# Attention with three heads instead of two between scores and values, and retention's first tiles in other rooms

## The chip, the cores and the metric

One core of one Trainium2 chip. The core has five engines that run their own instruction queues: PE (TensorE), DVE (VectorE), ACT (ScalarE), POOL (GpSimd) and SP (SyncE, here a queue that issues transfers). The metric is the device time of one execution in microseconds (us), as the median of several runs. Lower is better.

## The reference, cut to what matters

The program is one layer of a decoder with three branches (retention, pooling, sparse attention) for 1024 prompt tokens and 8 x 8 sample tokens. What the change touches is the prompt's attention and the beginning of retention:

```python
s_s = einsum('nqgrd,ngqsd->ngqrs', qb, k_selected) + bias_s     # 8 heads, 64 channels each
p_s = masked_softmax(s_s, dist >= 0)
o_s = einsum('ngqrs,ngqsd->nqgrd', p_s, v_selected)
s_w = einsum('nqgrd,nsgd->nqgrs', qb, k_window) + bias_w         # the last 512 positions
p_w = masked_softmax(s_w, valid_w)
o_w = einsum('nqgrs,nsgd->nqgrd', p_w, v_window)
o   = g0 * o_cmp + g1 * o_s + g2 * o_w
...
z = rms_norm(x, gain) @ w_in
q = rotary(q, pos); k = rotary(k, pos) * dk ** -0.5              # retention, 4 heads, chunks of 128
att = (q @ k.T) * dmask; o = att @ v + (q @ s) * cross; s = s * decay + (k * tail).T @ v
```

## The kernel before, in words

Every large product runs as three f16 products (high x high, high x low, low x high), so weights and activations are kept as pairs of f16 tiles, "h" and "l".

**Attention.** `prompt_attention` (L704) goes over 64 heads: 8 query tiles i of 128 rows, in each 8 heads (2 groups g of 4). With i the number of key blocks grows from 1 to 8 for the selected branch and from 1 to 5 for the window branch. For one head there are three steps.

- `head_scores` (L822): PE multiplies queries and keys into PSUM (L841, L853, L862), DVE adds the bias into an f32 tile `S` (L847, L873) and keeps the maxima, ACT makes the exponent's offset `nm` (L867).
- `head_probs` (L740), for the window branch first and then the selected one: ACT takes the exponentials (L750, L751), DVE or ACT writes their f16 half into `hl`, POOL subtracts to get the other half (L756), and SP issues a transposing transfer from `hl` to `pt` (L758), so that the keys come to lie on the partitions. `hl` and `pt` have 2 rooms for each branch (NHL, NPT).
- `head_values` (L766): PE multiplies `pt` by the values into `o` (L769 and L787, both by way of L1322 to L1324).

Step n of the loop holds the scores of head n, the values of head n - LAG, the weights of head n - 1 and then some steps of the generator `fill`. LAG is 2, and `S` has 3 rooms. After every fourth head `head_norm` (L876) divides on DVE and adds on POOL (L881 to L884); `head_out` (L887) turns that on PE (L891) and gates it. Once per query tile `cmp_attention` (L790) does the compressed branch.

**Fill.** `fill` is a chain of two projections of the input, `silu_c` for retention's gate and `early_gates` (L307 to L309). One step is three matmuls. They need nothing of the attention, and they stand between the heads so that PE has work; each output part goes through a small tile `th` (L932, L1200) of the pool `attw`, and that of `early_gates` from there to memory (`egd`, L1201). By the quota, 24 of the 360 steps are left behind the last head. They follow `head_out` in the program.

**Retention.** `retention` (L1124) loads the weights of its first head (`load_r`, L264, on the ACT queue, in 8 parts of 128 rows), then small tables and the table `rope` of sines and cosines (L1138, L1140, 1.1 MB, on the SP queue), and goes over 4 heads of 9 token tiles. For each, PE makes `z` (L286 to L288, 24 matmuls), `ret_tile` (L1223) rotates it on DVE (L1238 to L1240), after ACT has once per head scaled the table (L1233); SP turns the result (`qt`, L1256), and PE makes the chunk's scores `at` and, two stages later, the output `ro`. `z` has 3 rooms.

**Rooms.** Pools are stacked in SBUF; one that closes leaves its bytes to the next. Per partition, and above what stays: the attention's keys, queries and tables take the first 54.7 KB (`attc` 11.8, `attk` 32.8, `attb` 10.1), its working tiles `attw` lie above. After it, `smc` takes the first 12.4 KB, then come retention's weights `rw` (two rooms of a pair, 32.8 KB, to 45.1), its tables `rc` (23.2 KB, to 68.3; `rope` is 18.4 KB of that), and its working tiles. A tile in a reused room waits for the last user of just those bytes (`reuse_waits="tile"`).

**Order.** Each engine's queue runs in order. Which order that is, a planner decides when the program is built: by a model of the durations it takes, for each engine, the earliest instruction of the program that the model holds ready. So PE may have fill steps ahead of values that the model still waits for, and the order is kept on the chip whatever the true times are. `issue_after(x)` ties what follows to come behind x on x's engine.

Of the kernel before, what the change touches and what calls it, by code (L numbers as in the profile page):

```python
# [11 lines left out]
F32 = mybir.dt.float32  # L12
F16 = mybir.dt.float16
# [7 lines left out]
P = 128  # L21
# [5 lines left out]
N_EARLY, N_FILL = 8, 7  # L27
# [8 lines left out]

FILL_A, FILL_B = 0.2, 3.6

LAG = 2
ND = (1, 2, 3, 4, 5, 6, 7, 8)  # L40
NHL, NPT = 2, 2

# [20 lines left out]
C_RG = 2048  # L63
# [4 lines left out]
C_NG = 5400  # L68
# [59 lines left out]
class Kern:  # L128
# [32 lines left out]
    def run(self):  # L161
        ctx = self.ctx
        right = ExitStack()
        self.setup(ctx)
        with ExitStack() as es:
            self.kvstore(es)
            with ExitStack() as e1:
                self.phase_kv(e1)
            rp = self.pool(right, "gate", side="right")
            self.ga = rp.tile([P, 8, NG, 2, 32], F16, tag="ga", name="ga", bufs=1)  # L170
            self.rp = rp
            self.gc = rp.tile([P, 4, NG, 2, 32], F16, tag="gc", name="gc", bufs=1)
            with ExitStack() as e1:
                sp = self.pool(e1, "attw", bufs=2)
                ps = self.pool(e1, "aps", bufs=1, space=PSUM)
                self.pjb = A_PJ
                self.wq = self.nc.scalar
                self.eq = self.nc.scalar
                self.egd = self.dr.tile([8, P, NTOK], F32, name="egd")
                self.cgd = self.dr.tile([8, P, NTOK], F32, name="cgd")  # L180
                with self.behind():
                    deque(self.silu_c(sp, self.gc, C_NG, ps, self.wng), 0)
                fill = chain(self.silu_c(sp, self.ga, C_RG, ps), self.early_gates(sp, ps, range(N_FILL)))
                self.prompt_attention(sp, ps, fill)
                with self.tc.issue_after(self.after.ins):
                    deque(fill, 0)
                self.eq = self.nc.sync
        with ExitStack() as eo:
            self.smc = self.pool(eo, "smc")
            self.pjb = R_PJ  # L190
            with ExitStack() as es:
                self.psb, ppj, psa = [self.pool(es, x, bufs=1, space=PSUM) for x in ("rpsb", "rppj", "rpsa")]
                self.retention(es, ppj, psa, right)
            self.gbp = self.pool(right, "gbp", side="right")
            self.gb = self.gbp.tile([P, 4, NG, 2, 32], F16, tag="gb", name="gb", bufs=1)
            with ExitStack() as es:
                psb, ps, pst = [self.pool(es, x, bufs=1, space=PSUM) for x in ("spsb", "sppj", "spst")]
                sp = self.pool(es, "smp", bufs=1)
                pool = self.pooling(es, ps, pst)
                next(pool)  # L200
                with self.behind():
                    self.sample_attention(sp, psb, pst)
                next(pool, None)
                self.out_weights(self.pool(es, "wout"))
        with ExitStack() as es:
            self.output(es)
        right.close()
        if self.post:
            self.post(self)
# [53 lines left out]

    def load_r(self, pool, h):  # L264

        hi, lo = [pool.tile([P, 8, 512], F16, tag="rw" + x, name=self.nm("rw" + x), bufs=2) for x in "hl"]
        w = self.d["w_in"][0]
        for k in range(8):
            raw = self.wtile([P, 1024], F32, "raw")
            r = slice(k * P, k * P + P)  # L270
            qk = w[r, C_RET:C_RET + 1024].rearrange("p (a h c) -> p a h c", a=2, c=P)[:, :, h, :]
            self.wq.dma_start(raw[:, 0:256].rearrange("p (a c) -> p a c", c=P), qk)
            self.wq.dma_start(raw[:, 256:512], w[r, 1024 + h * 256:1280 + h * 256])
            self.wsplit(hi[:, k, :], lo[:, k, :], raw[:, :512])
        return hi, lo
# [25 lines left out]
    def proj_c(self, out, hi, lo, s0, n, ks=range(8)):  # L301

        nc = self.nc
        for k in ks:
            xh = self.xh[:, k, s0:s0 + n]
            xl = self.xl[:, k, s0:s0 + n]
            nc.tensor.matmul(out, hi[:, k, :], xh, start=(k == 0), stop=False)  # L307
            nc.tensor.matmul(out, hi[:, k, :], xl, start=False, stop=False)  # L308
            nc.tensor.matmul(out, lo[:, k, :], xh, start=False, stop=(k == 7))  # L309

    def evac(self, out, c0, ps, n, m):

# [387 lines left out]
    def prompt_attention(self, sp, ps, fill):  # L700

        order = range(8)
        heads = [(i, g, r) for i in order for g in range(2) for r in range(4)]
        sc, pr, out, oc = {}, {}, None, {}  # L704
        quota = 0.0
        for n in range(64 + LAG):
            if n < 64:
                sc[n] = self.head_scores(*heads[n], sp, ps)
            if n >= LAG:
                i, g, r = heads[n - LAG]  # L710
                if r == 0:
                    self.o = ps.tile([P, 2, 4, 64], F32, tag="o", name=self.nm("o"), bufs=A_O)
                s, nm, l = sc.pop(n - LAG)
                self.head_values(i, g, r, s, pr.pop(n - LAG), self.o, sp, ps)
                if r == 1 and out:
                    self.head_out(*out, sp, ps)
                if r == 3:
                    out = (i, g, self.head_norm(i, g, self.o, l, oc[i], sp))
            if 1 <= n <= 64:
                i, g, r = heads[n - 1]  # L720
                pr[n - 1] = self.head_probs(i, r, sc[n - 1], sp)
            if n < 64:
                i = heads[n][0]
                quota += FILL_A * (i + 1 + min(i + 1, 5)) + FILL_B
                with self.tc.issue_after(self.after.ins):
                    while quota >= 1:
                        next(fill, None)
                        quota -= 1
                if n % 8 == 3:
                    oc[i] = self.cmp_attention(i, sp, ps)  # L730
        self.head_out(*out, sp, ps)

    @staticmethod
    def cuts(i):
# [90 lines left out]
    def head_scores(self, i, g, r, sp, ps):  # L825
        nc = self.nc
        h = 4 * g + r
# [4 lines left out]
        near = min(2, i + 1) * P  # L832
        far_s, far_w = nk - near, nw - near
        nfs = -(-far_s // 512)
        s = sp.tile([P, 1664], F32, tag="S", name=self.nm("S"), bufs=3)

        st = sp.tile([P, 8], F32, tag="hst", name=self.nm("hst"), bufs=4)
        pn = ps.tile([P, 2, 256], F32, tag="s", name=self.nm("pn"), bufs=A_S)
        for br in range(2):
            for hl in range(2):  # L840
                self.after = nc.tensor.matmul(pn[:, br, :near], q, self.kst[:, br * 4 + g * 2 + hl, nk - near:nk],  # L841
                                 start=(hl == 0), stop=(hl == 1))
# [7 lines left out]
        if far_w:  # L850
            pw = ps.tile([P, 512], F32, tag="s", name=self.nm("pw"), bufs=A_S)
            for hl in range(2):
                nc.tensor.matmul(pw[:, :far_w], q, self.kst[:, 4 + g * 2 + hl, w0:w0 + far_w],  # L853
                                 start=(hl == 0), stop=(hl == 1 and i < 4))
# [3 lines left out]
        for c in range(nfs):  # L858
            n = min(512, far_s - 512 * c)
            pf = ps.tile([P, 512], F32, tag="s", name=self.nm("pf"), bufs=A_S)  # L860
            for hl in range(2):
                nc.tensor.matmul(pf[:, :n], q, self.kst[:, g * 2 + hl, 512 * c:512 * c + n], start=(hl == 0),  # L862
                                 stop=(hl == 1))
# [259 lines left out]

    def retention(self, es, ps, psa, right):  # L1124
        nc, d = self.nc, self.d
        rw = self.pool(es, "rw")
        rc = self.pool(es, "rc")
        rp = self.pool(es, "rp", bufs=2)
        lg = np.log1p(-np.exp2(-5.0 - np.arange(4)))
        w = {0: self.load_r(rw, 0)}  # L1130
        self.wq = nc.sync
        self.wp3 = self.pool(right, "wpipe3", side="right")
        rv = rc.tile([P, 2, 2, 4], F32, name="rv")
        nc.sync.dma_start(rv, d["c_rv"])

# [6 lines left out]
        nc.sync.dma_start(mt, d["c_mt"])  # L1142
        mts = rc.tile([64, 4, 64], F32, name="mts")
        nc.sync.dma_start(mts, d["c_mts"])
        c2 = rc.tile([P, 2, 4], F32, name="c2")
        nc.vector.tensor_tensor(c2, rv[:, :, 0, :], rv[:, :, 0, :], op=ALU.mult)
        nc.vector.tensor_scalar(c2, c2, 1.0 / 256, None, op0=ALU.mult)
# [13 lines left out]
        for n in range(len(steps) + NSTAGE):  # L1161
            z = None
            if n < len(steps):
                h, t = steps[n]
                z = ps.tile([P, 512], F32, tag="pj", name=self.nm("z"), bufs=self.pjb)
                self.proj_t(z, *w[h], t, 0, 512)
                if t == 2 and h < 3:
                    with self.behind():
                        w[h + 1] = self.load_r(rw, h + 1)

            for x in reversed(live):
                next(x, None)
            if z is not None:
                live.append(self.ret_tile(rp, psa, h, t, z, env))
            if n > 5:
                with self.behind():
                    next(prep, None)
            if n == len(steps) - 2:
                with self.behind():
                    self.raw0 = [self.sample_rows(self.smc, b) for b in range(2)]  # L1180
# [781 lines left out]
```

## Time and profile before

| | |
|---|---|
| three runs | 1325.66, 1319.22, 1324.78 us; median 1324.78 |
| the profiled execution | 1325.59 us, its span 1323.8 us |
| busy | PE 95%, DVE 68%, ACT 48%, POOL 39% of the span |
| TensorE's granted clock | 0.982 of full speed in the mean |
| prompt attention | about 158 to 507 us of the span |
| retention's first tiles | about 508 to 545 us |

The profile is one execution. A line of a timeline gives start, duration, engine, source line, operation, the tile written <- the tiles read, and in brackets for how long the engine stood before it and what released it. A line of waits gives who waited for whom, us in total, how often, and the longest.

### The profile page before, as it was taken

Reading aid. Unit: us, or ns where it says so; the run is one execution under the profiler, and the core shown is the slowest. Engines: PE = TensorE matmul, PEld = TensorE weight load, DVE = VectorE, ACT = ScalarE, POOL = GpSimd, SP = SyncE. Lnnn points to the kernel's source line nnn. Section 1 sums busy time; section 2 is a strip of 40 time slices with the busy share of each in tenths; the row PEclk is TensorE's granted clock in tenths of the full one; section 3 lists DMA queues with packets and bytes.
Section 4 is the critical chain, followed back from the end, with each engine's and each line's share of the span. In section 5 each row is a group of like instructions: output and inputs, shape, how many; then the busy total and the mean of one; then the engine's idle time right before and its main releaser. Section 6 shows DMA issues by size and latency. Waiting matters only on the chain. (4 is left out here: it accounts for less than half of the span.)

```text
span 1323.8 us, 27839 instructions
## 1 busy us (share of the span) xinstructions
PE 1260.5 (95%) x10520; PEld 853.9 (65%) x10520; DVE 905.6 (68%) x2288; ACT 632.3 (48%) x1474; POOL 518.6 (39%) x561
## 2 busy tenths in 40 slices
PE   7999899999999899899999998998999999999997
PEld 4555566767666664455656565666788888888643
DVE  6647536777767663767675657664588967579975
ACT  5633436766757662555554444344543433212332
POOL 1112013566665661245463560101534466423133
PEclk8999899999999999999999999998999999999998
DMA  7866624678889996252652278326641211543622
GB/s 258 171 129 153 143 64 95 108 134 151 165 156 182 167 189 178 61 151 68 174 133 61 63 212 249 104 50 226 220 144 33 81 49 49 170 138 116 230 97 97
DMA packets 324317, 179.25 MB, mean 135 GB/s; under 512 B 204434, under 2 KB 298610, under 8 KB 323765
## 3 DMA queue, kind: packets, MB, share of 16 engines
q1 hardware_dynamic: 283844, 137.83, 44.2%
q10 hardware_dynamic: 35600, 26.32, 6.8%
q0 software_dynamic: 4736, 13.31, 3.2%
q8 instruction: 82, 1.34, 0.4%
q14 instruction: 55, 0.44, 0.1%
HBM read 98.80 MB, written 33.25 MB: 100 GB/s over the span
## 5 line engine op out<-in xcount | busy, mean ns | idle before, releaser
L756 POOL TENSOR_TENSOR hl<-S,hl 128x640 f16<-128x640 f32 (+7 forms) x128 | 152.6, 1201 | 153.0 <-DVE hl L755 94.0
L307 PE MATMUL pj<-xh,whi 128*128 128x384 f16 (+1 forms) x480 | 154.1, 321 | 4.8 <-ACT ue L1417 4.1
L309 PE MATMUL pj<-xh,wlo 128*128 128x384 f16 (+1 forms) x480 | 153.9, 321 | 0.0
L308 PE MATMUL pj<-xl,whi 128*128 128x384 f16 (+1 forms) x480 | 153.8, 320 | 0.0
L286 PE MATMUL z<-rwh,xh 128*128 128x512 f16 x256 | 97.0, 379 | 0.0
L288 PE MATMUL z<-rwh,xl 128*128 128x512 f16 x256 | 97.0, 379 | 0.0
L287 PE MATMUL z<-rwl,xh 128*128 128x512 f16 x256 | 97.0, 379 | 0.0
L751 ACT ACTIVATE S<-S,nm 128x640 f32<-128x640 f32 (+7 forms) x128 | 93.7, 732 | 4.3 <-DVE gc L934 0.4
L308 PEld LDWEIGHTS <-whi 128*128 128x128 f16 x672 | 66.5, 99 | 38.6 <-issue 8.4
L309 PEld LDWEIGHTS <-wlo 128*128 128x128 f16 x672 | 66.5, 99 | 36.2 <-issue 2.4
L307 PEld LDWEIGHTS <-whi 128*128 128x128 f16 x672 | 66.4, 99 | 34.0 <-issue 2.4
L1566 DVE TENSOR_TENSOR q<-st,q 128x288 f32<-128x288 f32 (+1 forms) x168 | 70.3, 434 | 26.2 <-PE st L1557 25.2
L220 ACT ACTIVATE whi<-raw 128x1024 f16<-128x1024 f32 (+1 forms) x48 | 45.5, 948 | 63.8 <-PE pj L308 14.7
L286 PEld LDWEIGHTS <-xh 128*128 128x128 f16 x448 | 45.4, 101 | 46.2 <-issue 7.0
L1322 PE MATMUL o<-vst,pt 128*128 128x64 f16 x528 | 58.3, 194 | 17.6 <-DMA pt<-hl 17.2
L288 PEld LDWEIGHTS <-xl 128*128 128x128 f16 x448 | 44.1, 98 | 46.1 <-issue 2.1
L847 DVE CUSTOM_DVE_ANT_0 S<-pn,tnear 128x256 f32<-128x256 f32 (+1 forms) x128 | 47.3, 403 | 36.5 <-PE pn L841 32.2
L287 PEld LDWEIGHTS <-xh 128*128 128x128 f16 x448 | 44.0, 98 | 42.7 <-issue 1.8
L1322 PEld LDWEIGHTS <-pt 128*128 128x128 f16 x528 | 47.7, 98 | 26.9 <-DMA pt<-hl 23.4
L1254 POOL TENSOR_TENSOR rh<-rot,rh 128x256 f16<-128x256 f32 (+1 forms) x36 | 26.0, 721 | 96.9 <-ACT rh L1253 96.7
L308 PE MATMUL eg<-xl,whi 128*128 128x384 f16 (+1 forms) x192 | 62.0, 323 | 0.0
L309 PE MATMUL eg<-xh,wlo 128*128 128x384 f16 (+1 forms) x192 | 61.9, 322 | 0.0
(511 smaller groups left out, 4048.5 us busy)
## 6 DMA issues: line engine op xcount, KB each, us to landing
raw<-w_in SPq DMA_DIRECT2D x26, 512.0 KB
raw<-w_in ACTq DMA_DIRECT2D x18, 512.0 KB
raw<-w_in SPq DMA_DIRECT2D x48, 128.0 KB
wad<-q ACTq DMA_DIRECT2D x21, 256.0 KB
txd<-rso SPq DMA_DIRECT2D x8, 544.0 KB
raw<-egd SPq DMA_DIRECT2D x16, 272.0 KB
s<-state_ret SPq DMA_DIRECT2D x16, 256.0 KB
o_ret_s<-s POOLq DMA_DIRECT2D x16, 256.0 KB
```

The lines of the kernel that those rows point to most:

```text
L220: a = nc.scalar.activation(hi, raw, AF.Copy, scale=WS)
L286: nc.tensor.matmul(out, xh, hi[:, k, c0:c0 + n], start=(k == 0), stop=False)
L287: nc.tensor.matmul(out, xh, lo[:, k, c0:c0 + n], start=False, stop=False)
L288: self.marks["PE"] = nc.tensor.matmul(out, xl, hi[:, k, c0:c0 + n], start=False, stop=(k == 7))
L307: nc.tensor.matmul(out, hi[:, k, :], xh, start=(k == 0), stop=False)
L308: nc.tensor.matmul(out, hi[:, k, :], xl, start=False, stop=False)
L309: nc.tensor.matmul(out, lo[:, k, :], xh, start=False, stop=(k == 7))
L751: nc.scalar.activation(s[:, c0:c1], s[:, c0:c1], AF.Exp, bias=nm[:, br:br + 1], scale=0.125, accum_out=l[:, 0, br, r:r + 1])
L756: nc.gpsimd.tensor_tensor(hl[:, w:2 * w], s[:, d0:c1], hl[:, :w], op=ALU.subtract)
L847: nc.vector.tensor_tensor_reduce(out=outs[br], in0=pn[:, br, :near], in1=tn, scale=1.0, scalar=LOW, op0=ALU.add, op1=ALU.max, accum_out=st ...
L1322: nc.tensor.matmul(out, lhs[0], rhs[0], start=start, stop=False)
L1566: nc.vector.tensor_tensor(out[:, c0:c0 + n], b, x[:, c0:c0 + n], op=ALU.add)
```

## The change

Six edits. (1) LAG is 3: step n has the values of head n - 3. (2) `S` has LAG + 1 = 4 rooms. (3) The two users of `th` take it from a pool of its own, `atth`, that lies above `attw`. (4) Behind the last values six steps of `fill` come ahead of the last `head_out`, and that is tied behind the sixth; 18 steps stay for afterwards. (5) `rc` is allocated first, then two pools `rwa` and `rwb` for the weights with one room each, which the heads use in turn: the tables come to lie from 12.4 to 35.5 KB, the first head's weights from there to 51.9 KB, the second's to 68.3 KB. (6) The transfers of the tables stand ahead of the first weights' in the program.

```diff
-LAG = 2
+LAG = 3
...
                 sp = self.pool(e1, "attw", bufs=2)
+
+                tp = self.pool(e1, "atth")
...
-                    deque(self.silu_c(sp, self.gc, C_NG, ps, self.wng), 0)
-                fill = chain(self.silu_c(sp, self.ga, C_RG, ps), self.early_gates(sp, ps, range(N_FILL)))
+                    deque(self.silu_c(tp, self.gc, C_NG, ps, self.wng), 0)
+                fill = chain(self.silu_c(tp, self.ga, C_RG, ps), self.early_gates(tp, ps, range(N_FILL)))
...
-        hi, lo = [pool.tile([P, 8, 512], F16, tag="rw" + x, name=self.nm("rw" + x), bufs=2) for x in "hl"]
+        hi, lo = [pool.tile([P, 8, 512], F16, tag="rw" + x, name=self.nm("rw" + x), bufs=1) for x in "hl"]
...
-            nc.tensor.matmul(out, lo[:, k, :], xh, start=False, stop=(k == 7))
+            self.filled = nc.tensor.matmul(out, lo[:, k, :], xh, start=False, stop=(k == 7))
...
-        self.head_out(*out, sp, ps)
+        for _ in range(6):
+            next(fill, None)
+        with self.tc.issue_after(self.filled.ins):
+            self.head_out(*out, sp, ps)
...
-        s = sp.tile([P, 1664], F32, tag="S", name=self.nm("S"), bufs=3)
+        s = sp.tile([P, 1664], F32, tag="S", name=self.nm("S"), bufs=LAG + 1)
...
-        rw = self.pool(es, "rw")
+
         rc = self.pool(es, "rc")
+        rw = [self.pool(es, x) for x in ("rwa", "rwb")]
...
-        w = {0: self.load_r(rw, 0)}
-        self.wq = nc.sync
-        self.wp3 = self.pool(right, "wpipe3", side="right")
         rv = rc.tile([P, 2, 2, 4], F32, name="rv")
...
         nc.sync.dma_start(mts, d["c_mts"])
+        w = {0: self.load_r(rw[0], 0)}
+        self.wq = nc.sync
+        self.wp3 = self.pool(right, "wpipe3", side="right")
...
-                        w[h + 1] = self.load_r(rw, h + 1)
+                        w[h + 1] = self.load_r(rw[(h + 1) % 2], h + 1)
```

## Rows read from the trace of the kernel before

**Rows 1.** The page's first part: busy us, share of the span, instructions.
```profile
PE 1260.5 (95%) x10520; PEld 853.9 (65%) x10520; DVE 905.6 (68%) x2288; ACT 632.3 (48%) x1474; POOL 518.6 (39%) x561
```
**Rows 2.** PE's waits, whole span, then 487 to 560 us.
```profile
PE o L1322 <- DMA pt<-hl: 17.2, 21, 3.0
...
PE ro L1322 <- ACT ah L1269: 2.3, 1, 2.3
PE ro L1324 <- DVE al L1270: 1.4, 2, 0.8
PE to L891 <- POOL ob L884: 1.3, 1, 1.3
...
PE at L1322 <- DMA qt<-rh: 0.8, 1, 0.8
```
**Rows 3.** PE's waits for the turned weights, 400 to 450, then 450 to 505 us.
```profile
PE o L1322 <- DMA pt<-hl: 4.4, 3, 3.0
...
PE o L1322 <- DMA pt<-hl: 3.0, 4, 1.0
```
**Rows 4.** Windows of 5 us: length, busy by engine, PEclk, DMA share, GB/s.
```profile
385.00:390.00 5.00, 5.00 (x38) 3.21 (x39) 0.00 (x0) 2.44 (x4) 3.31 (x3) 0.69 0.93 185
...
435.00:440.00 5.00, 5.00 (x38) 2.92 (x35) 0.45 (x3) 2.44 (x4) 2.94 (x2) 0.66 0.88 168
...
535.00:540.00 5.00, 4.77 (x50) 3.74 (x46) 3.56 (x10) 2.40 (x7) 0.29 (x1) 0.67 0.39 103
```
**Rows 5.** Timeline: scores of the last two heads, then the last head's weights.
```profile
479.53 0.60 PE L841 MATMUL pn<-kst,qst 128*128 128x256 f16 x4
...
485.95 0.60 PE L841 MATMUL pn<-kst,qst 128*128 128x256 f16 x4
...
494.46 2.13 POOL L756 TENSOR_TENSOR hl<-S,hl 128x1024 f16<-128x1024 f32 x1 [0.91 <-ACT S L751]
...
496.62 3.08 SPq L758 DMA_TRANSPOSE pt<-hl  x1
```
**Rows 6.** Timeline of PE: last values and head_out; first matmuls of two fill steps.
```profile
488.81 0.20 PE L1322 MATMUL o<-vst,pt 128*128 128x64 f16 x1 [0.80 <-DMA pt<-hl]
...
498.18 0.20 PE L1322 MATMUL o<-vst,pt 128*128 128x64 f16 x1 [0.51 <-DMA pt<-hl]
...
498.79 0.33 PE L307 MATMUL eg<-xh,whi 128*128 128x384 f16 x1
...
499.27 0.33 PE L307 MATMUL eg<-xh,whi 128*128 128x384 f16 x1
...
508.13 0.44 PE L891 MATMUL to<-ident,ob 128*128 128x128 f32 x2 [1.32 <-POOL ob L884]
```
**Rows 7.** Timeline of the start of retention: the table, the first rotation, DVE's later stand.
```profile
514.10 0.94 SPq L1138 DMA_DIRECT2D rope<-c_rope  x2
...
519.34 0.42 DVE L1238 TENSOR_TENSOR rot<-z,rope 128x256 f32<-128x256 f32 x1 [7.51 <-ACT rope L1233]
...
527.67 0.69 DVE L221 SCALAR_TENSOR_TENSOR rwl<-raw,rwh 128x512 f16<-128x512 f32 x1 [3.39 <-ACT rwh L220]
```
**Rows 8.** Waits of SP's queue (160 to 225, then 150 to 560 us), of ACT (155 to 510).
```profile
SPq L758 <- PE o L1324: 27.2, 6, 12.8
...
SPq L1138 <- DMA egd<-th: 10.2, 2, 5.4
...
ACT hl L750 <- DMA pt<-hl: 11.8, 10, 2.4
```
**Rows 9.** Timeline: last part of the first weights is split; first matmul that needs it.
```profile
510.16 0.69 DVE L221 SCALAR_TENSOR_TENSOR rwl<-raw,rwh 128x512 f16<-128x512 f32 x1 [1.54 <-ACT rwh L220]
...
512.94 0.38 PE L286 MATMUL z<-rwh,xh 128*128 128x512 f16 x1
```
**Rows 10.** Transfers, 480 to 500 us: busy tenths in slices of 0.5 us; SP's queue.
```profile
DMA  9999999999990299999903999992999999129909
...
q1 hardware_dynamic: 11045, 2.78, 87.3%
```

## The prediction

> **What bounds the kernel now.** I read the page's first part: PE is busy 95% of the span and DVE, next, 68% [rows 1]. PE's work is the same before and after (no matmul is added or dropped), so the change can only take away time in which PE stands, 1323.8 - 1260.5 = 63.3 us, or time in which it runs at the low clock. I then read PE's waits: the largest is that for the turned weights, 17.2 us in 21 waits, the longest 3.0 [rows 2]. Then windows of 5 us around the longest stands, for the granted clock. After the two of about 3 us it is 0.69 and 0.66 in the next 5 us [rows 4]. Since only the levels 1.2 and 2.4 GHz occur, that is some 3 us at half speed. Last the timeline of one head, and that from the last head to retention's first tiles.
>
> **Why PE waits.** The last head's scores begin at 485.95; its last weights leave POOL at 494.46 + 2.13 = 496.6, and the turn is issued from 496.6 to 499.7 [rows 5]. So a head's weights are issued for turning only 10.7 to 13.8 us after its scores began, and the transfer's own time comes on top. Its values follow the scores of the second head after it: two heads last about 2 x 6.4 = 12.8 us [rows 5], and the values that PE reached at 488.81 - 0.80 = 488.0 [rows 6] stand 2.1 us behind the scores of 485.95. 14.9 us against 13.8 and a transfer: the two are level, and any delay of DVE or POOL shows as a stand of PE.
>
> **Three heads between.** One more head gives each turn up to 6.4 us more; the longest wait is 3.0. 7.4 of the 17.2 us lie behind 400 us, in the longest heads [rows 3]. Of the 17.2 us, 0.80 + 0.51 = 1.3 belong to the last values [rows 6]; the other **15.9** I take as gone. The least that goes, if the late part (4.4 + 3.0 - 1.3 = 6.1) stays, is 9.8. With the stands goes the low clock behind them: 5 x 0.31 + 5 x 0.34 = **3.3 us** [rows 4].
>
> The longer distance has a price in rooms. `pt` keeps two rooms, so the turn of head m now waits for the values of head m - 2 in the step of head m + 1, a head later than now. Those values are due right behind the scores of head m + 1, about 6.4 + 2.1 = 8.5 us after the scores of head m. The larger turn is ready at 10.7 and does not wait; the window's comes before it and may, but behind it on SP's queue stands only the larger one. I take 0 for it. The upper bound is the fourth rival's. The fourth room of `S` costs nothing and frees DVE earlier.
>
> **The end of attention.** The wait of 0.80 goes for the same reason as the others; that of 0.51 is for the very last head, which gains no time, and stays. The 1.32 us before the last `head_out` are POOL's adding [rows 6]. A fill step is 499.27 - 498.79 = 0.48 us, so six of them are 2.9 us of PE work behind the last values, more than the 1.3 lacking. Now the planner had put all 24 ahead of it and came out short, as the last values stood late; with the tie the wait should go, and if the planner again places the last values late, it stays. Gain 0.8 + 1.3 = **2.1** (0.8 to 2.6). In exchange one head's values more lie behind the last scores: no cost, as they only moved.
>
> **The start of retention.** The table's transfer waits on SP for `th`'s last transfer to memory, 10.2 us [rows 8], because its room reaches from 45.2 to 63.6 KB and so over the first tiles of `attw`. It is issued at 514.10, and DVE stands 7.51 us before the first rotation at 519.34 [rows 7]. All behind it on SP's queue (the sample's states, the turn of tile 0, the second head's weights) is late by as much, DVE stands again 3.39 us at 527.67 behind those weights, and PE pays 2.3 + 1.4 + 0.8 = 4.5 us [rows 2] and then a clock of 0.67 for 5 us, 5 x 0.33 = 1.65 [rows 4]. In its new place the table lies over keys and queries, which are free after the last scores (begun at 485.95, over by some 487). Even behind all turns on SP's queue it is issued at about 500 and, with the 5.2 us from issue to first use [rows 7], is there before tile 0 is through. I take 4.0 of the 4.5 and the whole 1.65 as gone: **5.7** (0 to 6.2).
>
> What it takes: 1.1 MB of table now move while the last turns and the first head's weights move. The last part of those weights is ready at 510.16 + 0.69 = 510.85 and needed at 512.94 [rows 9]; that slack of 2.1 us shrinks by the 1.3 us that PE comes earlier, to 0.8. A table of 1.1 MB held the transfers for up to 5.2 us [rows 7], so a stand of 0 to 4.4 us; I take **1.0**, near the low end: the last parts are asked for behind 500, when a table that goes at 487 has passed.
>
> **New waits of the new order.** Every queue is planned anew. Nothing in the trace shows that; by the small waits that the present order leaves (0.5 to 0.8 each, [rows 2, 6]) I allow **1.5** (0 to 5).
>
> **Sum.** -15.9 - 3.3 - 2.1 - 5.7 + 1.0 + 1.5 = -24.5. Against the profiled execution's own 1325.6 that gives 1301.1; it lies 0.8 above the median, less than the scatter of the runs (6.4), so I leave it at **1301**.
>
> **Rivals.**
>
> *The transfers are the bound in the late heads.* A head of i = 7 turns 512 + 320 = 832 KB. From 480 to 500 SP's queue alone was busy 87.3% [rows 10]. If heads can't come faster than their turns, the late waits [rows 3] (6.1 without the last two) and the second clock loss (1.7) stay, and with them small ones: 1301 + 8 = **1309**. For it: nearly all slices of rows 10 read 9. Against it: some read 0 to 3, so the queue runs dry between bursts, though it moved 139 GB/s, gaps included. The Trainium skill ("DMA: Bandwidth & Descriptors", "Latency and other measured facts") gives 261 GB/s for such a transfer; by that a head's turns would take an estimated 3.2 us, far below a head's length, and this rival would fall.
>
> *The table gets in front of the last turns.* It is free to go at some 487, when the last two heads' turns are not yet issued, and it stands in the same queue. If the planner puts it there, the last turns come up to 5.2 us later [rows 7], PE stands for most of it and falls to the low clock (1.65): 1301 + 6.9 = **1308**. Against it: 24 fill steps, 11.5 us, lie there for cover. The Trainium skill ("DMA: Bandwidth & Descriptors", "Queues, rings and completion order") says that each transfer engine takes a queue's descriptors in ring order, and that a completion signal lands only after the earlier writes. By that rule the turns would wait out the table in full, and the time is this rival's.
>
> *Slower: the rooms.* If the planner puts values behind the fill steps of their step (3 us), the turn of head m, held by the `pt` room, lands later than ACT wants the same `hl` room for head m + 2. ACT then stands, the fill's results stay in their two PSUM rooms, and PE stops. SP has waited so 27.2 us in 6 waits from 160 to 225 us, ACT 11.8 in 10 waits already [rows 8]. It decides once a turn lands more than two heads (12.8 us) and the way from scores to exponential after its scores; now it is issued by 13.8. Price: 1.2 us (11.8 / 10) in each of the 32 heads of i >= 4, 38 us: 1301 + 38 = **1339**. Against it: those waits of SP lie in the first heads, and ACT's longest is 2.4 us.
>
> *It doesn't do what it says.* The planner gives the won head away (values placed as early as its model allows), and the 19 waits stay: only the end and retention gain, 1325.6 - 2.1 - 5.7 + 1.0 = **1319**.
>
> **How the numbers follow.** Forecast 0.62, transfers bound 0.11, table in front 0.13, order gives it away 0.08, slower 0.06. A measurement of this kernel can tell about 0.5% (6.6 us) from no change. The first three lie below 1318: faster 0.86; the fourth counts as same, 0.08; slower 0.06. Range: the low end is all gains at their bounds, 15.9 + 3.3 + 2.6 + 6.2 = 28.0, so 1297.6, less half of the runs' scatter: 1294. The high end takes in 1309 with the upper bounds of the new waits (3.5 + 3.4): 1316. Left out: the last two rivals and the extremes.
>
> **What would show it.** Right: no wait for turned weights above 1 us from 225 to 485, granted clock 1.00 behind 380 and 430; the table issued before 501, no DVE stand over 2 us before the first rotation; PE's busy time unchanged near 1260. Wrong: PE waiting for `pt` behind 400 as now (transfers), a stand over 2 us at the last values or in the first `z` (table in front), ACT standing at L750 for more than 20 us (rooms), or new waits of retention's output `ro`.

## The result and the profile after

Median 1308.4 us against 1323.9 for the kernel before, measured side by side: ratio 0.9897, 95% interval 0.9865 to 0.993, some 13.6 us by the ratio (the two medians lie 15.5 apart). Faster by more than the 0.5% that a measurement can tell; forecast were 1301 and a gain of 24.5. The profiled execution took 1306.29 us, the fastest of its five runs, while that of the kernel before, 1325.59, lies at the slow end of its own (1316.08 to 1325.66); so the two traces differ by 19.3 us, more than the kernels do.

The page's first part after, the answer to [rows 1]:

```profile
PE 1251.3 (96%) x10520; PEld 850.6 (65%) x10520; DVE 912.2 (70%) x2288; ACT 631.3 (48%) x1474; POOL 525.2 (40%) x561
```

PE's instructions are the same in number; its busy time fell by 9.2 us (the prediction wanted it unchanged near 1260), 3.3 of it in the attention. To see where the time went, I cut both traces at the same four events: the first scores, the last scores, the first `z`, the last `z`. Windows of the kernel before, for these three stretches (length, busy by engine, PEclk, DMA share, GB/s):

```profile
157.80:487.60 329.80, 312.80 (x3435) 223.18 (x3433) 219.92 (x744) 208.56 (x477) 177.96 (x170) 0.99 0.72 135
487.60:508.40 20.80, 18.17 (x214) 12.84 (x210) 9.98 (x19) 9.28 (x17) 7.57 (x6) 1.00 0.90 199
508.40:755.00 246.60, 238.15 (x1543) 133.42 (x1541) 161.79 (x471) 126.30 (x363) 104.76 (x162) 0.99 0.40 108
```

The same three of the changed kernel:

```profile
156.70:471.70 315.00, 306.46 (x3393) 220.64 (x3392) 227.93 (x742) 207.14 (x476) 181.60 (x168) 1.00 0.78 141
471.70:498.40 26.70, 21.17 (x254) 14.54 (x251) 11.35 (x25) 12.05 (x21) 9.30 (x8) 0.94 1.04 226
498.40:739.80 241.40, 236.42 (x1543) 132.22 (x1542) 160.39 (x467) 123.82 (x361) 105.33 (x162) 1.00 0.40 105
```

The heads up to the last scores: -14.8 us. From there to the first `z`: +5.9. Retention's projections: -5.2. One head's values moved from the first stretch to the second (254 matmuls there against 214, about 1.3 us), so the heads gained 13.5 and the end lost 4.6. Behind the last `z` to the end of the span lie 568.8 us before (1323.8 - 755.0) and 564.7 after (1304.5 - 739.8). No edit changes the instructions of that part; in all the profiles of this study it lies between 563.5 and 571.1, so I read those 4 us as scatter (the last section shows where it arises).

PE's waits for turned weights before, 225 to 300, 300 to 400 and 400 to 485 us:

```profile
PE o L1322 <- DMA pt<-hl: 4.7, 9, 1.2
...
PE o L1322 <- DMA pt<-hl: 5.2, 5, 2.9
...
PE o L1322 <- DMA pt<-hl: 6.1, 5, 3.0
```

After, in the same three windows, and then from 485 to 560:

```profile
PE o L1328 <- DMA pt<-hl: 4.0, 7, 1.7
...
PE o L1328 <- DMA pt<-hl: 1.8, 2, 1.3
...
PE o L1328 <- DMA pt<-hl: 0.5, 1, 0.5
...
PE o L1328 <- DMA pt<-hl: 4.2, 2, 3.9
PE to L896 <- POOL ob L889: 1.3, 1, 1.3
```

In the long heads, behind 300 us, the waits are all but gone (11.3 to 2.3); in the shorter heads ahead of 300 they stayed; and a new one of 3.9 stands at the last values. The granted clock of these two traces goes the same way. The windows that read 0.69, 0.66 and 0.67 in [rows 4] are at full clock, and a low stretch is new behind the stand:

```profile
385.00:390.00 5.00, 5.00 (x91) 4.12 (x90) 4.06 (x15) 4.01 (x8) 4.01 (x4) 1.00 0.47 84
435.00:440.00 5.00, 5.00 (x64) 3.60 (x63) 4.72 (x13) 3.61 (x8) 2.99 (x4) 1.00 1.19 268
485.00:490.00 5.00, 2.51 (x43) 1.89 (x44) 1.38 (x2) 1.64 (x3) 0.00 (x0) 0.86 1.26 262
490.00:495.00 5.00, 5.00 (x48) 3.24 (x47) 0.85 (x2) 1.86 (x4) 0.00 (x0) 0.80 0.69 202
535.00:540.00 5.00, 5.00 (x32) 2.75 (x30) 4.59 (x16) 3.76 (x13) 2.15 (x5) 1.00 0.12 27
```

The timeline there: the table's transfers on SP's queue, the turn behind them, then PE's stand and, against [rows 7], DVE's first rotation:

```profile
474.67 1.12 SPq L1141 DMA_DIRECT2D rope<-c_rope  x2
475.90 12.59 SPq L763 DMA_TRANSPOSE pt<-hl  x3
...
487.23 0.20 PE L1328 MATMUL o<-vst,pt 128*128 128x64 f16 x1 [3.90 <-DMA pt<-hl]
...
503.86 0.42 DVE L1244 TENSOR_TENSOR rot<-z,rope 128x256 f32<-128x256 f32 x1 [1.71 <-PE z L290]
```

The table is issued ahead of the last three turns, which hold the queue for 12.6 us. The first of them, issued at 475.90, is the second to last head's larger turn, and PE can use it only at 487.23, 11.3 us later.

The rooms, as SP's wait for PE's values (225 to 485 us) and ACT's for `hl` (225 to 500), before:

```profile
SPq L758 <- PE o L1324: 3.3, 3, 1.9
...
ACT hl L750 <- DMA pt<-hl: 6.6, 7, 2.1
```

and after:

```profile
SPq L763 <- PE o L1330: 36.7, 18, 8.8
...
ACT hl L755 <- DMA pt<-hl: 26.7, 20, 3.6
```

### The profile page after: what moved, and what is told of

It reads as the page before. It is cut to its first block, busy times and chain, and to the rows that moved or that the text cites. A ratio compares the mean times of both kernels' runs of the same rounds, so it can differ in the third digit from the quotient of the medians.

```text
span 1304.5 us, 27795 instructions
## 1 busy us (share of the span) xinstructions
PE 1251.3 (96%) x10520; PEld 850.6 (65%) x10520; DVE 912.2 (70%) x2288; ACT 631.3 (48%) x1474; POOL 525.2 (40%) x561
## 5 line engine op out<-in xcount | busy, mean ns | idle before, releaser
L1572 DVE TENSOR_TENSOR q<-st,q 128x288 f32<-128x288 f32 (+1 forms) x168 | 70.3, 433 | 26.4 <-PE st L1563 25.3
L755 ACT ACTIVATE hl<-S,nm 128x128 f16<-128x128 f32 (+7 forms) x64 | 49.1, 767 | 36.6 <-DMA pt<-hl 36.5
L1328 PE MATMUL o<-vst,pt 128*128 128x64 f16 x528 | 56.3, 193 | 10.7 <-DMA pt<-hl 10.6
L760 DVE CAST hl<-S 128x640 f16<-128x640 f32 (+4 forms) x64 | 33.2, 519 | 45.9 <-ACT S L756 16.2
L309 PE MATMUL eg<-xh,whi 128*128 128x384 f16 (+1 forms) x192 | 61.5, 320 | 0.0
```

Source lines behind the costliest of these rows:

```text
L755: nc.scalar.activation(hl[:, :w], s[:, d0:c1], AF.Exp, bias=nm[:, br:br + 1], scale=0.125)
L1328: nc.tensor.matmul(out, lhs[0], rhs[0], start=start, stop=False)
L1572: nc.vector.tensor_tensor(out[:, c0:c0 + n], b, x[:, c0:c0 + n], op=ALU.add)
```

## The experiments

Every row below is one kernel: its distance, rooms of `S` and of `pt`, where the table lies on SP's queue, the measured ratio to the kernel before, and from its profile the attention (first scores to first `z`, of which the end from the last scores on) and retention (first to last `z`), us.

| kernel | LAG | S | pt | table | median us | ratio (95%) | attention | of it the end | retention |
|---|---|---|---|---|---|---|---|---|---|
| before | 2 | 3 | 2 | late | 1320.6 to 1323.9 | 1 | 350.6 | 20.8 | 246.6 |
| after | 3 | 4 | 2 | in front | 1308.4 | 0.9897 (0.9865 to 0.993) | 341.7 | 26.7 | 241.4 |
| distance and room alone | 3 | 4 | 2 | late | 1314.8 | 0.9941 (0.992 to 0.9961) | 339.7 | 24.3 | 247.3 |
| moves alone | 2 | 3 | 2 | in front | 1318.2 | 0.9965 (0.9941 to 0.999) | 352.1 | 25.3 | 242.5 |
| two between, four S | 2 | 4 | 2 | in front | 1319.0 | 0.9984 (0.9967 to 1.0001) | 352.4 | 24.5 | 241.3 |
| three S | 3 | 3 | 2 | in front | 1315.2 | 0.9959 (0.9939 to 0.9979) | 347.0 | 28.1 | 241.4 |
| three pt, three S | 3 | 3 | 3 | in front | 1306.7 | 0.9881 (0.9857 to 0.9904) | 341.4 | 27.9 | 243.1 |
| window's third pt | 3 | 4 | 3 and 2 | in front | 1307.4 | 0.9879 (0.984 to 0.9919) | 341.4 | 26.6 | 242.8 |
| half turn | 3 | 4 | 2 | in front | 1307.8 | 0.9876 (0.9825 to 0.9927) | 342.8 | 26.2 | 240.8 |
| big table behind | 3 | 4 | 2 | part behind | 1309.4 | 0.9907 (0.9884 to 0.993) | 345.5 | 27.5 | 241.3 |
| fill ahead | 3 | 4 | 2 | in front | 1312.3 | 0.9905 (0.9872 to 0.9938) | 346.0 | 27.1 | 241.4 |
| tables behind | 3 | 4 | 2 | behind | 1307.9 | 0.9893 (0.9874 to 0.9912) | 339.7 | 22.3 | 242.0 |
| both ties | 3 | 4 | 2 | behind | 1309.4 | 0.9901 (0.9881 to 0.992) | 338.3 | 22.4 | 243.9 |
| both ties, window's third pt | 3 | 4 | 3 and 2 | behind | 1303.6 | 0.9859 (0.9836 to 0.9883) | 337.0 | 23.2 | 243.4 |

Median and ratio come from 4 to 12 runs, the three stretches from one profiled execution each, which can lie some us off its median (three pt: 1312.0 against 1306.7).

**The distance and its rooms.** First the distance, with the fourth room of `S`, on the kernel before:

```diff
-LAG = 2
+LAG = 3
...
-        s = sp.tile([P, 1664], F32, tag="S", name=self.nm("S"), bufs=3)
+        s = sp.tile([P, 1664], F32, tag="S", name=self.nm("S"), bufs=LAG + 1)
```

> The kernel before with three heads between and the fourth score room alone: retention's rooms, the six fill steps and the silu rooms as before. If the attention is worth what the two traces differ by (waits 15.9 to 7.8, clock 3.3: 11.4 us) and the values' end gains its 0.8: 1323.9 - 12.2 = 1311.7, ratio 0.991, and the stand of 3.9 us at the last values is not there, since the table's transfer still comes behind. DVE stands 7.5 us ahead of the first rotation as in the kernel before. Rival (the distance alone gives little, the rooms of retention give most): 1318 or more, with waits for turned weights of 12 us or more from 160 to 485 us.

It gave less, 0.9941. The heads did what they do in the changed kernel:

```profile
156.40:471.80 315.40, 307.23 (x3395) 220.66 (x3394) 227.51 (x744) 207.06 (x476) 181.99 (x168) 1.00 0.78 141
471.80:496.10 24.30, 20.54 (x252) 14.69 (x249) 13.44 (x22) 10.69 (x20) 10.11 (x8) 0.93 0.86 181
496.10:743.40 247.30, 239.53 (x1543) 133.41 (x1542) 160.79 (x469) 126.61 (x362) 104.96 (x162) 0.99 0.40 107
```

so the heads' gain is that of the distance and its room, and retention's (246.6 to 241.4) is not. Not as expected: a stand of 3.8 us at the last values is there without any table in front. Some seven fill steps stand ahead of it in PE's queue, and nine follow behind it.

Then the fourth room undone, in the changed kernel:

```diff
-        s = sp.tile([P, 1664], F32, tag="S", name=self.nm("S"), bufs=LAG + 1)
+        s = sp.tile([P, 1664], F32, tag="S", name=self.nm("S"), bufs=3)
```

> The changed kernel with three rooms of S in place of four. My prediction held the fourth room at nothing beyond freeing DVE earlier: 1308 +- 2, ratio 0.988, waits for turned weights from 160 to 485 us of 6 to 8 us. Rival (with three heads between, the fourth room is what lets the scores run ahead): PE waits for a room of S or of its scores' PSUM, the head's steps lengthen, 1313 or more.

The rival holds: 0.9959, and its interval begins at 0.9939, above 0.993 where the changed kernel's ends. Lastly the room without the distance (`LAG = 2`, four rooms of `S`):

> The changed kernel with two heads between and four rooms of S. So far: two heads and three rooms 0.9965, three heads and three rooms 0.9959, three heads and four rooms 0.9897. Theory one (the room is what pays, since with it DVE writes scores before POOL is through with the oldest head): 1311, ratio 0.991, waits for turned weights well under the 22.0 us of two heads and three rooms. Theory two (distance and room pay together alone: with two heads between PE waits for turns however early DVE is): 1316 to 1319, ratio 0.996, waits for turned weights 18 to 24 us. By my prediction, which gave the room no price, theory two holds and the room alone changes nothing.

Theory two holds: 0.9984. So of the four combinations of heads between and rooms of `S`, with the moves made and two rooms of `pt`, two and three give 0.9965, two and four 0.9984, three and three 0.9959, three and four 0.9897: by the medians neither the distance nor the room measurably pays alone. (The one profile of the distance with three rooms does show attention 5.1 us shorter than with two between, 347.0 against 352.1; its runs as a whole don't bear it out.) PE's waits for turned weights over the whole span, with two between and three rooms, and with two between and four:

```profile
PE o L1328 <- DMA pt<-hl: 22.0, 24, 3.4
```

```profile
PE o L1328 <- DMA pt<-hl: 21.6, 24, 2.9
```

With two between the extra room changes nothing, as PE waits for the turns. With three between and three rooms these waits are down to 10.4, but others come (5.6 us for POOL's sums at `head_out`, 1.0 of the scores for DVE), and the heads take 318.9 instead of 315.0 us. Which single instruction the missing `S` room delays, no row settles; it stays open.

The rooms of `pt`: a third for both branches, for which `S` has to go back to three, and then a third for the window's turns alone, with four of `S`:

```diff
-NHL, NPT = 2, 2
+NHL, NPT = 2, 3
...
-        s = sp.tile([P, 1664], F32, tag="S", name=self.nm("S"), bufs=LAG + 1)
+        s = sp.tile([P, 1664], F32, tag="S", name=self.nm("S"), bufs=3)
```

> The changed kernel with three rooms of pt in place of two, and three of S in place of four, since four and three don't fit. Rooms theory (a turn waits for values two heads back, and ACT behind it for hl): ACT's standing at the exponential for hl falls from 36.5 us to under 15, SP's for PE's values from 52 to under 15, PE's waits for turned weights from 160 to 485 us from 6.4 to under 3: 1308.4 - 4 = 1304, ratio 0.985. Transfers' theory: those waits stay at 5 to 7 us and the time at 1308. If the third S room costs, the run with three S rooms alone shows it.

```diff
-                t = sp.tile([P, (10, 2 * max(ND))[br == 0], P], F16, tag=f"pt{br}", name=self.nm("pt"), bufs=NPT)
+                t = sp.tile([P, (10, 2 * max(ND))[br == 0], P], F16, tag=f"pt{br}", name=self.nm("pt"), bufs=NPT + br)
...
-        st = sp.tile([P, 4, 8], F32, tag="st", name=self.nm("st"))
+        st = sp.tile([P, 4, 8], F32, tag="st", name=self.nm("st"), bufs=1)
```

> The changed kernel with a third room of pt for the window's turns alone; four rooms of S stay, and a small tile of the compressed branch gets one room in place of two. Rooms theory (the window's turn waits for the values two heads back, and the larger one and ACT queue behind it): SP's waits for PE's values from 225 to 485 us fall from 36.7 to under 10, ACT's for hl from 26.7 to under 15, PE's for turned weights up to 485 from 6.4 to under 3, heads stage 315.0 to 312: 1305 to 1306, ratio 0.987. Transfers' theory: the standing moves from PE's values to the turns' landing, the heads stage stays within 1 us, 1308.

Waits of SP's queue (225 to 485 us), ACT (225 to 485) and PE (160 to 485) with three rooms of `pt` and three of `S`:

```profile
SPq L763 <- PE o L1330: 10.0, 4, 6.2
...
ACT hl L755 <- DMA pt<-hl: 13.4, 11, 3.0
...
PE o L1328 <- DMA pt<-hl: 2.1, 4, 0.9
```

Its fair counterpart is the kernel with three rooms of `S` and two of `pt`:

```profile
SPq L763 <- PE o L1330: 40.1, 18, 8.8
...
ACT hl L755 <- DMA pt<-hl: 25.6, 22, 3.1
...
PE o L1328 <- DMA pt<-hl: 5.5, 8, 1.5
```

The waits went as the rooms theory said, and the ratio from 0.9959 to 0.9881, intervals apart: with three between and three rooms of `S`, two rooms of `pt` do cost. The window's room alone, beside four of `S`, did about half as much (SP's wait 23.3, ACT's 20.1, PE's unchanged at 6.4), less than was expected of it, and its 0.9879 can't be told from the changed kernel's 0.9897. A third room of `pt` with two heads between was not run.

**The transfers.** Half the turned bytes; this kernel leaves the low halves of the weights out of the values:

```diff
-                nc.sync.dma_start_transpose(t[:, :2 * w // P], hl[:, :2 * w])
+                nc.sync.dma_start_transpose(t[:, :w // P], hl[:, :w])
...
-            self.mm3(o[:, 1, r, :], (turned[1][:, b, :], turned[1][:, nw + b, :]), (v[:, 0], v[:, 1]), b == 0, b == nw - 1)
+            self.mm3(o[:, 1, r, :], (turned[1][:, b, :], turned[1][:, b, :]), (v[:, 0], v[:, 1]), b == 0, b == nw - 1)
...
-            self.mm3(o[:, 0, r, :], (t[:, b - np_, :], t[:, nd + b - np_, :]), (v[:, 0], v[:, 1]), b == 0, b == ns - 1)
+            self.mm3(o[:, 0, r, :], (t[:, b - np_, :], t[:, b - np_, :]), (v[:, 0], v[:, 1]), b == 0, b == ns - 1)
```

> The changed kernel with only the high halves of the weights turned: half the bytes of every turn, the same number of matmuls (PE reads the high half where it read the low one, so the low halves of the weights are left out of the values). Transfers' theory (the late heads and the end of attention are bound by what the turns, the first weights and the table move): waits for turned weights from 160 to 485 us fall from 6.4 to under 1, last scores to first z from 26.7 to 22, DMA share from 350 to 480 from 1.04 to some 0.6, 1298, ratio 0.982. Rooms or order theory: the turns come sooner, but the rooms' rule and PE's order stay, the waits fall by less than half, 1304 to 1307.

From 350 to 400 us the DMA share fell to 0.74, and PE's waits over the whole span stayed (the half turn first, then the changed kernel):

```profile
350.00:400.00 50.00, 48.77 (x595) 35.04 (x592) 38.74 (x117) 34.62 (x71) 34.49 (x27) 1.00 0.74 124
...
350.00:400.00 50.00, 48.15 (x602) 34.90 (x603) 36.41 (x115) 35.69 (x70) 34.37 (x26) 1.00 1.04 189
```

```profile
PE o L1328 <- DMA pt<-hl: 10.8, 9, 2.8
...
PE o L1328 <- DMA pt<-hl: 10.6, 12, 3.9
```

The transfers' theory falls: a DMA share over 1 in the late heads is load, not the bound. (The turns of this kernel don't wait for POOL's halves either, so they were free to go earlier still.)

**The end of attention.** The moves alone (`LAG = 2` in the changed kernel, so three rooms of `S`):

> The changed kernel with two heads between and three rooms of S: the edits of retention, of th and of the fill steps alone. In the two traces the stretch of retention fell by 5.2 us (246.6 to 241.4), the heads up to the last scores by 14.8, the stretch from there to the first z rose by 5.9. If these parts are independent: 1321.1 - 5.2 = 1316, ratio 0.996, waits for turned weights of some 17 us as in the kernel before, and no DVE stand over 2 us ahead of the first rotation. Rival (the table and the last turns share the transfers, so that the end of attention pays what retention gains): last scores to first z over 24 us where the kernel before has 20.8, time 1319 to 1322.

```profile
157.50:484.30 326.80, 308.75 (x3428) 221.63 (x3426) 219.77 (x742) 208.22 (x477) 177.41 (x169) 1.00 0.73 138
484.30:509.60 25.30, 20.07 (x218) 13.72 (x215) 9.89 (x25) 11.61 (x21) 7.73 (x6) 0.93 1.03 221
...
PE o L1328 <- DMA pt<-hl: 17.5, 21, 2.2
```

Both came: retention gains 4.1 us (242.5), and the end of attention, 20.8 before, loses 4.5. With two between, too, the moves lose at the end of attention what they win in retention. Yet the ratio is 0.9965, its interval below 1, and in this trace the heads, into which of the moves only that of `th` reaches, took 326.8 us where the kernel before took 329.8. Their waits are no shorter (last line, 160 to 485 us: 17.5, before 15.9); but their granted clock is 1.00 throughout, and the two low windows of [rows 4] are not there. The moves were tested only together, so which of them brings retention's gain is open. To undo the cause of the loss at the end, I tied the two large transfers of the table behind the last turn:

```diff
-                nc.sync.dma_start_transpose(t[:, :2 * w // P], hl[:, :2 * w])
+                self.turned = nc.sync.dma_start_transpose(t[:, :2 * w // P], hl[:, :2 * w])
...
-        for t in (0, 4):
+        with self.tc.issue_after(self.turned.ins):
+            for t in (0, 4):
```

> The changed kernel, with the two large transfers of retention's table tied behind the last turn of weights. Theory one (the table in front of the last three turns makes PE stand): the waits for turned weights from 485 us on fall from 4.2 us to under 1, the low clock behind them goes (1.8), retention starts as before: 1308.4 - 3.4 - 1.8 = 1303, ratio to the kernel before 0.984. Rival (the last turns are late by themselves, by the two rooms of pt or the transfers): PE stands some 3 us at the last values all the same, 1307 to 1309. Second rival: the table comes too late, DVE stands over 2 us ahead of the first rotation and retention's start loses up to the 5.7 us that it gained: 1308 to 1309, but with the stand in another place.

A miss: 0.9907, 6.3 us of stands at the last values. But the tie left three small tables between the last turns on SP's queue, so it did not make the clean comparison, and what those stands wait out is not shown. Nor did it help to move fill ahead, with the table in front:

```diff
-                self.head_values(i, g, r, s, pr.pop(n - LAG), self.o, sp, ps)
+                with self.tc.issue_after(self.filled.ins) if n > 64 else ExitStack():
+                    self.head_values(i, g, r, s, pr.pop(n - LAG), self.o, sp, ps)
+                for _ in range((0, 9, 9, 0)[max(0, n - 63)]):
+                    next(fill, None)
```

> The changed kernel with the values of the last two heads tied behind nine fill steps each on PE; the table stays in front of the last turns. Order theory (PE stands 3.9 us for the turn of the second to last head while 13 fill steps stand behind it in its queue): the stands at the last values fall from 4.2 us to under 1.5 and the low clock behind them goes, last scores to first z 26.7 to 22 or 23, 1304, ratio 0.986. Rival (the end is bound by the landing of the last turn and what follows it, values, division, sum, head_out): PE stands as long a head later or at head_out, the stretch stays at 25 to 27 us, 1307 to 1309.

PE stood 4.5 us at the same turn and the end took 27.1. The landing sets it, as the rival said, and not the fill. With `issue_after` around all the tables (`rope`, `mt`, `mts`):

> The changed kernel with all of retention's tables, the three small ones too, tied behind the last turn of weights; PE's order is then that of the run with the distance alone, give or take a fill matmul. Theory (the table in front of the last turns in SP's queue holds their landing): the stretch from the last scores to the first z falls from 26.7 to 24.3 us, as in the run with the distance alone, one stand of about 3.8 us stays (the window's turn of the last head, with fill behind it in PE's queue), retention keeps its 241.4: 1308.4 - 2.4 = 1306, ratio 0.987. Rival (turns, first weights and table share the same transfers in any order): the stretch stays at 26 to 27.5 us or DVE stands over 2 us ahead of the first rotation, 1308 to 1309.

```profile
475.50:497.80 22.30, 19.48 (x252) 13.81 (x249) 11.84 (x25) 10.35 (x19) 9.75 (x8) 1.00 1.09 240
497.80:739.80 242.00, 236.51 (x1543) 132.27 (x1542) 161.03 (x467) 126.14 (x365) 104.98 (x162) 1.00 0.40 108
...
479.77 2.95 SPq L763 DMA_TRANSPOSE pt<-hl  x1
...
485.81 0.20 PE L1329 MATMUL o<-vst,pt 128*128 128x64 f16 x1 [1.12 <-DMA pt<-hl]
```

The end is 4.4 us shorter than the changed kernel's, at full clock and with no stand over 1.3 us at the values, where 3.8 had been expected to stay. The second to last head's larger turn is usable 6.0 us after its issue, with PE standing for it, where it took 11.3 behind the table. Retention keeps its gain (DVE's longest stand for a rotation is 2.2). The ratio, 0.9893 against 0.9897, does not show these 4 us; they are read from one execution of each kernel. With the fill ahead as well:

> Both ties together: all tables behind the last turn, and the values of the last two heads behind nine fill steps each. If the table holds the turns and the rest of the loss is fill that stands behind a stand in PE's queue: the second to last head's turn lands within 9 us of the last scores and doesn't stop PE, the last one stops it for some 3 us, last scores to first z 22.5, 1304, ratio 0.985. Rival (the chain from the last scores over exponentials, halves, turn, division and sum sets the end by itself): the stretch stays at 24 us or more, 1306 to 1308.

The second to last head's larger turn is issued at nearly the same time as in the changed kernel (476.09), and its values run with no stand; the longest stand is now for POOL's sum ahead of `head_out`:

```profile
476.09 1.84 SPq L766 DMA_TRANSPOSE pt<-hl  x1
...
481.95 0.19 PE L1332 MATMUL o<-vst,pt 128*128 128x64 f16 x1
...
494.47 0.44 PE L899 MATMUL to<-ident,ob 128*128 128x128 f32 x2 [2.57 <-POOL ob L892]
```

The values of 481.95 begin with the window's turn; those of the larger one follow at 482.4, so it took at most 6.3 us. The end is 22.4, as expected; the total, 0.9901 where 0.985 was expected, again does not resolve it. Over all profiles with three heads between and the moves made, the end is 26.2 to 28.1 us in the seven kernels with the table, or part of it, ahead of the last turns, and 22.3 to 23.2 in the three with all of it behind, with or without fill ahead. (The distance alone, with its stand of 3.8 us, lies between: 24.3.)

**Together.** Both ties and the window's third room:

> The same two ties and the third room of pt for the window's turns: a try for a version that beats both kernels. In one profile the third room brought the heads to 314.8 us (changed kernel 315.0) with ACT's standing for hl at 20.1 in place of 26.7, so it is worth 0 to 2 us; the end as in the run with both ties, 22.5: 1302 to 1304, ratio 0.984. Rival (the room only lets the scores run further ahead of the turns, and PE stands at the end for it): 1305 to 1307.

```profile
156.70:470.50 313.80, 305.43 (x3393) 220.35 (x3392) 227.69 (x742) 206.06 (x476) 179.73 (x168) 1.00 0.78 143
470.50:493.70 23.20, 19.34 (x255) 14.05 (x252) 12.09 (x25) 10.57 (x19) 9.29 (x8) 1.00 1.11 239
493.70:737.10 243.40, 238.09 (x1543) 132.73 (x1541) 160.77 (x467) 125.45 (x364) 104.32 (x162) 0.99 0.39 106
```

1303.6 us, as expected, 0.9859: the fastest of the study, and some 5 us under the changed kernel. The two intervals overlap a little (0.9883 and 0.9865), so that it beats the changed kernel is likely and not shown.

## Why the prediction was right or wrong

Direction and range held; the gain was oversized, 24.5 against 13.6 us (15.5 by the medians). Of the two traces:

- **The waits in the heads, -15.9.** PE's waits for turned weights up to 485 us went from 15.9 to 6.4, -9.5, close to the lower bound of 9.8, but for the opposite reason. That bound let the late waits stay; they went (11.3 to 2.3 behind 300 us). What stayed lies ahead of 300 us (4.7 to 4.0, the longest 1.7 where none above 1 was to be left). The step that failed is "one more head gives each turn up to 6.4 us more", worked out from the last heads alone and taken for all. In part the head that was won went into waiting for a room: from 225 to 300 us SP's queue stood 2.3 us for PE's values before and 12.5 after, and with three rooms of `S` a third one of `pt` took PE's waits in all heads from 5.5 to 2.1.
- **The rooms of `pt`, 0.** The mechanism was described, the price was wrong: SP's wait for PE's values went from 3.3 to 36.7 us, and a third room was worth 0.8% with three rooms of `S`. As the rival of 1339 this came true in kind, not in size: its sign, ACT standing at `hl` for more than 20 us, is there (26.7).
- **The fourth room of `S`, "costs nothing".** It was no by-product. Without it, and with two rooms of `pt`, the medians show no gain from the distance; with a third room of `pt` they do (0.9881).
- **The clock, -3.3.** The two late windows are at full clock, but that this is the distance's doing is not shown; luck may have had a part. The two kernels with the moves and two heads between also have full clock throughout the heads, with 17.5 and 17.7 us of waits, the longest 2.2 and 2.0; the low windows of the kernel before come behind waits of 2.9 and 3.0 in one execution, at the slow end of its runs. And three profiles with three between have a low window in the heads (0.66, 0.68 and 0.73). Against the moves alone, whose heads ran at full clock, the heads of the changed kernel gained 10.5 us (326.8 - 315.0 - 1.3), not 13.5. About 1.4 us came back behind the new stand (2.51 x 0.14 + 5 x 0.20).
- **The end of attention, -2.1.** Wrong: +4.6. The rival with the table in front happened at the place it named; it was given a chance of 0.13 and priced at 6.9 us, and from -2.1 to +4.6 is 6.7. (That its total, 1308, is also the measured median is luck: the heads fell short of the forecast too.) Tying the tables behind took 4.4 off the end. The argument against it, 24 fill steps for cover, failed: PE's order had been fixed by a model, and with the table in front the turn took 11.3 us to land, longer than the fill that stood ahead. The rule of the Trainium skill cited there ("DMA: Bandwidth & Descriptors", "Queues, rings and completion order") fits: 11.3 us behind the table, 6.0 without it. The wait at `head_out` stayed (1.28 us). The six fill steps that edit 4 puts behind the last values changed nothing: in the kernel before, too, 18 fill matmuls, six steps, stood there (504.20 to 506.81), and in both kernels `head_out` followed the last values by 3.6 to 3.9 us.
- **The start of retention, -5.7 + 1.0.** Right: -5.2. DVE stands 1.7 instead of 7.5 us ahead of the first rotation; the stand of `z` for the first weights, priced at 1.0, did not come. The new waits of the new order, +1.5, can't be told apart from the rest.
- **The transfers as the bound.** It fell, shown by half the bytes. The estimate from the figure of the Trainium skill ("DMA: Bandwidth & Descriptors", "Latency and other measured facts") had said so; the busy slices of [rows 10] had not.

In sum for the attention 341.7 - 350.6 = -8.9 where -15.9 - 3.3 - 2.1 + 1.5 = -19.8 was forecast; retention as forecast.

## What to carry to other kernels

A longer distance between a producer and its consumer needs room in the buffers that it stretches: here it paid with a fourth room of `S` or with a third of `pt`, and by the medians not without either. Read the waits by stretch before calling them gone, since the same line can vanish in long steps and stay in short ones. Check the state of the clock in both traces before booking its loss to the change. When a load becomes free earlier, look at what stands behind it in its queue at that new time, and tie it behind whatever must not wait.

## What the runs showed of the hardware that I had not expected

The queue share of [rows 10], 87.3%, and a DMA share above 1 looked like a full transfer path, yet halving the bytes of every turn left PE's waits at 10.8 us (10.6 after). And the part behind the last `z`, whose instructions no edit changes, took 563.5 to 571.1 us from profile to profile: a spread of 7.6 us, wider than most of the effects studied here. It goes with TensorE's granted clock. Its first 100 us and PE's longest wait in them, before and after:

```profile
755.00:855.00 100.00, 95.83 (x707) 61.28 (x705) 69.95 (x175) 46.45 (x110) 32.87 (x41) 0.98 0.67 193
PE pj L307 <- ACT ue L1417: 4.1, 1, 4.1
...
739.80:839.80 100.00, 97.92 (x741) 62.98 (x738) 70.99 (x180) 47.24 (x112) 33.96 (x41) 1.00 0.66 190
PE pj L309 <- ACT ue L1423: 2.1, 1, 2.1
```

In seven of the 14 profiles this stretch is at 1.00, and the part takes 563.5 to 564.9 us; in the other seven it is at 0.97 or 0.98, and the part takes 567.0 to 571.1. PE's longest wait in it is 0.8 to 3.2 us in the former and 2.5 to 4.1 in the latter; why it differs from execution to execution stays open. The stretches of one trace show such effects, the medians only in part.
